# Moving the small tiles: weights at multiples of 512 bytes of a partition, turned activations 128 bytes beyond one

## Chip, cores and metric

The kernel runs on one core of one Trainium2 chip. The metric is the device time of one execution, in microseconds (us). All times of the kernel before come from three runs and from one profiled execution.

## What is computed

Two blocks of a network, each two layers deep, on 256 tokens of width 1024, in float32. The first block is an attention layer and a state-space (SSM) layer, each followed by a squared-ReLU MLP of width 4096. The second block has two layers, each a three-branch mixer followed by a mixture of 32 experts (MoE). Nearly all of the work is dense products of activations with weights that are read once from HBM:

```python
def first_block(x, ...):
    for i in range(DEPTH):
        mix = attention_mixer(...) if i % 2 == 0 else mamba2_bidir_mixer(...)
        x = layer_norm(DN_ALPHA * x + mix, ...)
        x = layer_norm(DN_ALPHA * x + jnp.square(jax.nn.relu(x @ w1)) @ w2, ...)

def second_block(x, c, positions, ...):
    for l in range(DEPTH):
        h = modulate(rms_norm(x, norm1_g[l]), sh1, sc1)
        x = x + gt1[:, None, :] * token_mixer(h, ...)
        h = modulate(rms_norm(x, norm2_g[l]), sh2, sc2)
        x = x + gt2[:, None, :] * hier_moe(h, ...)
    return rms_norm(x, final_g)
```

(The loops are written shorter here than in the reference.)

## The kernel before

**Stages.** The program runs attention, MLP 0, SSM, MLP 1, mixer 0, MoE 0, mixer 1, MoE 1 and the final norm, one after the other. `Stream` (`K.ws`) loads the weights of all stages in the order of use into a ring of five `raw` tiles of 1 MB. Outside the MoE each half of a `raw` tile is split into a high part `hi` (ScalarE, L160) and a rest `lo` (VectorE, L162), both of type float32r, in rings of seven tiles each. The activations are turned (transposed on TensorE, L368) and split in the same way by `tsplit` (L371, L372), into pairs that end in `h` and `l`.

**The two kinds of matmul.** A float32 product is made of three float32r matmuls: high by high, high by rest, rest by high.

- *Wide* ones (`mm3`, L266 to L268): 128 turned activations are loaded into the array (LDWEIGHTS) and up to 512 columns of a weight tile stream past them.
- *Narrow* ones (`b_half`, L339 to L341): 128 columns of a weight tile are loaded and 256 turned activations stream past.

Each matmul has a LDWEIGHTS of its own, and the one for the next matmul runs while the present matmul streams. So TensorE reads two places of SBUF at once: the one that streams and the one that is loaded. In the following, the *start* of a tile is its byte address in a partition modulo 512. All slices that these matmuls take of a tile begin at multiples of 512 bytes from the tile's own start (a few in the mixer at 256), so the start of the tile tells that of the slice. The *distance* is the difference of the two starts.

**Where the tiles lie.** Pools are laid out one after another in each partition, and every tile begins at a multiple of 32 bytes. Below the first pool lie 16384 bytes that the runtime keeps and four constants of 32 bytes each, so the first pool, the ring (L211 of the kernel before), begins 128 beyond a multiple of 512. `raw`, `hi` and `lo` have sizes that are multiples of 512 and keep that start. The pool `tail` (`self.tp`, L215) holds the tiles `th` and `tl` and behind them small tiles of the norms: `lnst` and `lnag` (L429, L430), `rstd` (L420) and `rss` (L1110, L1964). Behind it each stage opens a pool of its own, which begins 128 beyond a multiple of 512. In attention the row `sinkr` of 32 bytes lies ahead of the pair `xT` (L602, L606), in the mixer the row `fb` of 32 bytes (16 used; L1261, L1264), and so both pairs start at 160.

**Order of the work.** The program is written in the order of dependence, and a scheduler sets the order on each engine. The two loads `sinkr` and `fb` are DMAs that SyncE (SP) issues.

Of the kernel before, what the change touches and what calls it, by code (L numbers as in the profile page):

```python
# [10 lines left out]
F32 = mybir.dt.float32  # L11
# [19 lines left out]
class Job:  # L31
# [4 lines left out]
    def __init__(self, src, nk, ncol, nsplit, whole=False):  # L36
        self.src, self.nk, self.ncol, self.nsplit, self.whole = src, nk, ncol, nsplit, whole
        self.raw = None
        self.spare = self.pair = False
# [168 lines left out]
class Kern:  # L208
    def __init__(self, ctx, tc, ins, raw_bufs=5, split_bufs=7):
        self.ctx, self.tc, self.nc, self.I = ctx, tc, tc.nc, ins  # L210
        self.ring = ctx.enter_context(tc.tile_pool(name="ring", bufs=1, reuse_waits="tile"))  # L211
        self.cst = ctx.enter_context(tc.tile_pool(name="cst", bufs=1, reuse_waits="tile"))
        self.xp = ctx.enter_context(tc.tile_pool(name="xp", bufs=1, reuse_waits="tile"))
        self.rp = ctx.enter_context(tc.tile_pool(name="rows", bufs=1, reuse_waits="tile"))
        self.tp = ctx.enter_context(tc.tile_pool(name="tail", bufs=1, reuse_waits="tile"))  # L215
        self.ps = ctx.enter_context(tc.tile_pool(name="ps", bufs=1, space=PSUM))
        self.ready = {}
        self.finish = self.last = None
        self.held = 0
        self.actx = ExitStack()  # L220
        self.ws = Stream(self, raw_bufs, split_bufs)
        self.sides = []
# [193 lines left out]
    def rstd(self, var, eps, name="rstd"):  # L416

        nc = self.nc
        n = var.shape[1]
        r = self.tp.tile([128, 16], F32, name=name, tag=name, bufs=2)  # L420
        nc.vector.tensor_scalar(r[:, :n], var, eps, None, op0=OP.add)  # L421
        self.pow = nc.gpsimd.tensor_tensor(r[:, :n], r[:, :n], self.mhalf[:, :n], OP.pow).ins  # L422
        return r

    def layer_norm_tok(self, tok, P, g, b):

        nc = self.nc
        y = self.x[:, tok]
        st = self.tp.tile([128, 2, 6], F32, name="lnst", tag="lnst", bufs=2)  # L429
        ag = self.tp.tile([128, 2], F32, name="lnag", tag="lnag", bufs=2)  # L430
        for c in range(2):
            s = slice(c * 512, c * 512 + 512)
            nc.vector.scalar_tensor_tensor(y[:, s], y[:, s], ALPHA, P[c], op0=OP.mult, op1=OP.add)
            nc.vector.bn_stats(st[:, c], y[:, s])
        nc.vector.bn_aggr(ag, st)
        r = self.rstd(ag[:, 1:2], 1e-5)
        for c in range(2):
            s = slice(c * 512, c * 512 + 512)
            nc.vector.scalar_tensor_tensor(y[:, s], y[:, s], ag[:, 0:1], g[:, s], op0=OP.subtract, op1=OP.mult)
            i = nc.vector.scalar_tensor_tensor(y[:, s], y[:, s], r[:, 0:1], b[:, s], op0=OP.mult, op1=OP.add)  # L440
        self.last = i.ins
        return i.ins
# [151 lines left out]
def attn_layer(K):  # L594
    nc, tc, I, ws = K.nc, K.tc, K.I, K.ws
    with ExitStack() as ctx:
        p = ctx.enter_context(tc.tile_pool(name="att", bufs=1, reuse_waits="tile"))
# [1 line left out]
        c1 = p.tile([128, _C.shape[1] - nc1], F32, name="c1")  # L599
        nc.scalar.dma_start(c1, I["consts"][:, nc1:])  # L600
        win, rcos, rsin = (c1[:, _OFF[k][0] - nc1:_OFF[k][0] - nc1 + _OFF[k][1]] for k in ("win", "rcos", "rsin"))
        sinkr = K.load_row(p, I["attn_sink"][0], 8, "sinkr")  # L602
        K.place(p, ("sm", 2, 3, F32), ("smT", 2, 2, F32), ("nab", 4, 3, F32), ("ao", 8, 1, F32), ("qa", 4, 1, F32),
                ("qaT", 4, 1, F32), ("qbT", 4, 1, F32), ("kbT", 4, 1, F32), ("vb", 4, 1, F32))
        g, b = K.row(I["ln1_g"][0]), K.row(I["ln1_b"][0])
        xT = K.pair(p, 8, "xT")  # L606
        qa = p.tile([128, 2, 4, 2, 64], F32, name="qa")
        ka = p.tile([128, 2, 2, 64], F32, name="ka")
        va = p.tile([128, 2, 128], F32, name="va")
# [12 lines left out]
        for t in range(2):  # L622
            ct, st = rcos[:, t * 64:t * 64 + 64], rsin[:, t * 64:t * 64 + 64]
# [483 lines left out]
def rms_gain(K, tok, dst, sq, g, eps=1e-6):  # L1107

    nc = K.nc
    ss = K.tp.tile([128, 2], F32, name="rss", tag="rss", bufs=2)  # L1110
    K.squared = nc.scalar.activation(sq, K.x[:, tok], AF.Square, scale=D ** -0.5, accum_out=ss[:, 0:1]).ins
    for c in range(2):
        s = slice(c * 512, c * 512 + 512)
        K.gained = nc.vector.tensor_tensor(dst[:, s], K.x[:, tok, s], g[:, s], OP.mult).ins
    return K.rstd(ss[:, 0:1], eps)
# [132 lines left out]
def mixer_layer(K, l):  # L1248
    nc, tc, I, ws = K.nc, K.tc, K.I, K.ws
    with ExitStack() as ctx:  # L1250
        p = ctx.enter_context(tc.tile_pool(name="mix", bufs=1, reuse_waits="tile"))
# [6 lines left out]
                nc.sync.dma_start(shift, bass.AP(tensor=K.mod[l].tensor, offset=K.mod[l].offset, ap=[[0, 128], [1, D]]))  # L1258
        hn = p.tile([128, 2, D], F32, name="hn", tag="mg")
        K.place(p, ("gt", 4, 1, F32), ("rv", 4, 1, F32))  # L1260
        fb = K.load_row(p, I["fox_fb_2"][l], 4, "fb")  # L1261
        gq = K.load_row(p, I["mla_q_norm_g_2"][l], 256, "gq", tag="qpeT")
        gkv = K.load_row(p, I["mla_kv_norm_g_2"][l], 128, "gkv")
        hT = K.pair(p, 8, "xT")  # L1264

        def norm(t):
            tail = K.finish
            with ExitStack() as order:
                if t == 0:
                    order.enter_context(K.early(t, AHEAD))  # L1270
                elif tail:
                    order.enter_context(tc.issue_after(K.diag))
                    order.enter_context(tc.issue_after(K.turned))
                    tail(t)
                    K.finish = None
                r = rms_gain(K, t, hn[:, t], p.tile([128, D], F32, name="rsq", tag="yb"), gain)
                if t:
                    rms_scale(K, hn[:, t], r, shift)
                    K.tsplit(hn[:, t], hT, t, 0, 8)
                    end, turned = K.split  # L1280
                else:
                    with tc.issue_after(K.scattered) if l else nullcontext():
                        Ps = shift_pair(K, shift)
                    end = rms_pair(K, t, hn[:, t], r, shift, hT, p.tile([128, 8, 64], F32, name="dg", tag="rq", bufs=1)[:, 0:2].rearrange("p a b -> p (a b)"), Ps)
            if l == 0:
                K.release(t, end, turned if t else K.turned)
            elif tail:
                ws.limit = 1 << 30 if t else ws.limit + NEXT // 2
                with tc.issue_after(end), tc.issue_after(turned if t else K.squared):
                    ws.pump()  # L1290
# [19 lines left out]
        ss = p.tile([128, 4], F32, name="mss")  # L1310
# [4 lines left out]
        r = K.rstd(ss, 1e-6)  # L1315
# [636 lines left out]
def final_norm(K, dst):  # L1952
    nc = K.nc
    with ExitStack() as ctx:
        p = ctx.enter_context(K.tc.tile_pool(name="fin", bufs=1, reuse_waits="tile"))
        g = K.row(K.I["final_g_2"])
        o = p.tile([128, 2, D], F32, name="fo")
        c0, c1 = slice(0, 512), slice(512, 1024)
        for t in range(2):
            with K.tc.issue_after(i) if t else nullcontext():  # L1960
                if t and K.finish:
                    K.finish(t)
                    K.finish = None
                ss = K.tp.tile([128, 2], F32, name="rss", tag="rss", bufs=2)  # L1964
                nc.scalar.activation(p.tile([128, D], F32, name="rsq", tag="rsq", bufs=2), K.x[:, t], AF.Square, scale=D ** -0.5,  # L1965
                                     accum_out=ss[:, 0:1])
                i = nc.vector.tensor_tensor(o[:, t, c0], K.x[:, t, c0], g[:, c0], OP.mult).ins  # L1967
                r = K.rstd(ss[:, 0:1], 1e-6)
            nc.scalar.activation(o[:, t, c0], o[:, t, c0], AF.Identity, scale=r[:, 0:1])
            nc.vector.scalar_tensor_tensor(o[:, t, c1], K.x[:, t, c1], r[:, 0:1], g[:, c1], op0=OP.mult, op1=OP.mult)  # L1970
            for c in (c0, c1):
                nc.sync.dma_start(dst[0, t * 128:t * 128 + 128, c], o[:, t, c])
# [9 lines left out]
def program(ctx, tc, ins, out, phases=ALL, opts=None):  # L1982
# [24 lines left out]
    if "attn" not in phases:  # L2007
        with tc.tile_pool(name="set2", bufs=1) as p:
            setup2(K, p)
    run = {"attn": lambda: attn_layer(K), "mlp0": lambda: mlp_layer(K, 0), "mlp1": lambda: mlp_layer(K, 1), "ssm": lambda: ssm_layer(K),  # L2010
           "mix0": lambda: mixer_layer(K, 0), "mix1": lambda: mixer_layer(K, 1), "ada": lambda: ada_alone(K),
           "moe0": lambda: moe_layer(K, 0), "moe1": lambda: moe_layer(K, 1), "fin": lambda: final_norm(K, out)}
    for ph in phases:
        run[ph]()
# [32 lines left out]
```

## Time and profile before

| what | us |
|---|---|
| median of 3 runs | 2350.51 |
| lowest and highest | 2349.61, 2353.59 |
| the profiled execution, its own time | 2345.05 |
| its span, first to last instruction | 2343.3 |

| engine | busy us | share of the span |
|---|---|---|
| PE (matmul) | 2198.4 | 94% |
| PEld (weight load) | 1510.0 | 64% |
| DVE | 1180.4 | 50% |
| ACT | 811.4 | 35% |
| POOL | 118.7 | 5% |

The shares are averages over stages of different kinds; a matmul's recorded duration reaches into the next one, since matmuls are pipelined. How often matmuls start is read from the start times of the timeline, and not from a mean duration. The mean granted clock of TensorE was 0.987 of full speed.

### The profile page before, as it was taken

To read this page: it belongs to the slowest core of one execution; us is meant where nothing else is said; L and a number is where in the kernel's file an instruction comes from. 1 tells how busy PE (TensorE), PEld (TensorE's weight loads), DVE (VectorE), ACT (ScalarE), POOL (GpSimd) and SP (SyncE) were. 2 spreads that over 40 slices of the span, in tenths; PEclk is the share of its full clock that TensorE was granted. 3 is DMA by queue.
4 is the path that set the end of the run, shared out by engine and by line. 5 is a ranking of instruction groups with operands and counts; after the bars stand their busy time and mean duration, and the time that the engine had idled before them with its cause. 6 is when DMAs were issued, how large, how long until landed. Compare 5 with 4: busy or idle time off the path is not lost. (4 is left out here: it accounts for less than half of the span.)

```text
span 2343.3 us, 30480 instructions
## 1 busy us (share of the span) xinstructions
PE 2198.4 (94%) x11877; PEld 1510.0 (64%) x11877; DVE 1180.4 (50%) x2024; ACT 811.4 (35%) x1404; POOL 118.7 (5%) x98
## 2 busy tenths in 40 slices
PE   8999999998999999999999988889999899888887
PEld 7878889997888888874444443348877544443333
DVE  6589978997998756652111111036665411111113
ACT  5544446775444444431111111115443211111111
POOL 0000002222000000110000000000001000000000
PEclk9999999999999999998999999989999999999999
DMA  9379855434898554677999999985566899999997
GB/s 332 110 252 359 305 158 153 130 132 141 305 347 299 179 162 161 226 240 290 375 393 395 394 394 394 393 314 193 170 207 208 316 362 395 395 395 393 393 394 268
DMA packets 307105, 669.11 MB, mean 286 GB/s; under 512 B 20996, under 2 KB 60780, under 8 KB 306952
## 3 DMA queue, kind: packets, MB, share of 16 engines
q1 hardware_dynamic: 299496, 663.56, 78.2%
q10 hardware_dynamic: 7456, 3.49, 0.6%
q8 instruction: 97, 1.59, 0.3%
q14 instruction: 56, 0.46, 0.1%
HBM read 665.90 MB, written 1.10 MB: 285 GB/s over the span
## 5 line engine op out<-in xcount | busy, mean ns | idle before, releaser
L162 DVE TENSOR_TENSOR lo<-raw,hi 128x1024 fp32r<-128x1024 f32 (+2 forms) x353 | 433.5, 1236 | 184.5 <-ACT hi L160 183.1
L160 ACT ACTIVATE hi<-raw 128x1024 fp32r<-128x1024 f32 (+2 forms) x353 | 369.6, 1056 | 340.9 <-PE acc L268 224.9
L1712 PE MATMUL acc<-raw,XT 128*64 128x512 f32 x1248 | 366.5, 603 | 76.0 <-DMA raw<-in_exp_w 75.9
L1712 PEld LDWEIGHTS acc<-raw,XT 128*64 128x64 f32 x1248 | 109.8, 138 | 311.4 <-issue 179.3
L266 PE MATMUL acc<-hi,xTh 128*128 128x512 f32 (+2 forms) x608 | 229.5, 379 | 4.9 <-ACT xTh L371 2.4
L1712 PE MATMUL acc<-pre,XT 128*64 128x512 f32 x784 | 231.8, 597 | 0.0
L1727 DVE TENSOR_TENSOR aT<-s,acc 128x256 f32<-128x256 f32 x60 | 25.1, 422 | 410.3 <-ACT s L1725 409.8
L267 PE MATMUL acc<-lo,xTh 128*128 128x512 f32 (+2 forms) x608 | 226.6, 373 | 0.0
L268 PE MATMUL acc<-hi,xTl 128*128 128x512 f32 (+2 forms) x608 | 225.1, 374 | 0.4 <-DVE xTl L1150 0.3
L1740 PE MATMUL pb<-pre,aT 128*64 128x512 f32 x928 | 208.7, 594 | 0.0
L1764 DVE SCALAR_TENSOR_TENSOR Yl<-pb,wcol,Yh 128x512 fp32r<-128x512 f32 x56 | 40.2, 748 | 296.9 <-ACT Yh L1763 296.0
L1717 ACT ACTIVATE H<-acc 128x512 f32<-128x512 f32 x64 | 38.2, 597 | 382.4 <-PE acc L1712 382.4
L1740 PEld LDWEIGHTS pb<-pre,aT 128*64 128x64 f32 x928 | 80.3, 137 | 123.3 <-issue 115.3
L339 PE MATMUL acc<-xTh,hi 128*128 128x256 f32 x456 | 130.6, 287 | 2.9 <-DVE ca L895 2.9
L266 PEld LDWEIGHTS acc<-hi,xTh 128*128 128x128 f32 x608 | 115.5, 190 | 26.7 <-ACT xTh L371 4.1
L340 PE MATMUL acc<-xTl,hi 128*128 128x256 f32 x456 | 129.9, 285 | 0.0
L341 PE MATMUL acc<-xTh,lo 128*128 128x256 f32 x456 | 129.5, 285 | 0.0
L339 PE MATMUL pb<-xTh,hi 128*128 128x256 f32 x448 | 126.8, 285 | 1.4 <-ACT hi L160 1.4
L267 PEld LDWEIGHTS acc<-lo,xTh 128*128 128x128 f32 x608 | 115.5, 190 | 19.4 <-DVE lo L162 0.8
L268 PEld LDWEIGHTS acc<-hi,xTl 128*128 128x128 f32 x608 | 114.6, 190 | 20.6 <-DVE xTl L372 1.1
L340 PE MATMUL pb<-xTl,hi 128*128 128x256 f32 x448 | 126.7, 283 | 0.0
L422 POOL TENSOR_TENSOR rstd<-rstd,mhalf 128x1 f32<-128x1 f32 (+2 forms) x36 | 30.4, 845 | 1901.5 <-DVE rstd L421 1858.1
(493 smaller groups left out, 3920.0 us busy)
## 6 DMA issues: line engine op xcount, KB each, us to landing
pre<-in_exp_w SPq DMA_DIRECT2D x428, 512.0 KB
raw<-in_exp_w SPq DMA_DIRECT2D x160, 1024.0 KB
raw<-in_mlp_w SPq DMA_DIRECT2D x64, 1024.0 KB
adaw<-in_ada_w SPq DMA_DIRECT2D x96, 512.0 KB
raw<-in_w_in SPq DMA_DIRECT2D x24, 1024.0 KB
raw<-in_gate_w SPq DMA_DIRECT2D x24, 1024.0 KB
raw<-in_ssm_w_in SPq DMA_DIRECT2D x16, 1024.0 KB
raw<-in_branch_w SPq DMA_DIRECT2D x12, 1024.0 KB
```

The lines of the kernel that those rows point to most:

```text
L160: nc.scalar.activation(hi[:, :size], flat, AF.Copy)
L162: eng.tensor_tensor(lo[:, :size], flat, f32(hi[:, :size]), OP.subtract)
L266: nc.tensor.matmul(P, ah, bh, start=start, stop=False)
L267: nc.tensor.matmul(P, ah, bl, start=False, stop=False)
L268: nc.tensor.matmul(P, al, bh, start=False, stop=stop)
L339: nc.tensor.matmul(P, wh, xh[:, k + kk], start=first and start and kk == 0, stop=False, skip_group_check=True)
L340: nc.tensor.matmul(P, wh, xl[:, k + kk], start=False, stop=False, skip_group_check=True)
L341: nc.tensor.matmul(P, wl, xh[:, k + kk], start=False, stop=stop and kk == n - 1, skip_group_check=True)
L1712: K.pe = nc.tensor.matmul(P[64 * o:64 * o + 64], XT[G][1][k][:, i], hs[2 * o + u].raw[:, kk], start=(k == 0), stop=(k == 7)).ins
L1717: nc.scalar.activation(H[e], P, AF.Copy)
L1740: K.pe = nc.tensor.matmul(PY[c][64 * o:64 * o + 64], aT[2 * n + o][:, f], hs[2 * o + u].raw[:, 0, cs], start=(f == 0), stop=(f == 3)).ins
L1764: nc.vector.scalar_tensor_tensor(Y[j][1][:, cs], PY[c], wcol[:, j:j + 1], f32(Y[j][0])[:, cs], op0=OP.mult, op1=OP.subtract)
```

## The change

A pool `small` is opened ahead of the ring and takes the small tiles of the norms out of `tail`. It is 384 bytes long, so the ring begins at a multiple of 512, and the pools of the stages stay where they were, since `tail` is shorter by the same 384 bytes. In attention and in the mixer the pair `xT` is allocated ahead of the 32-byte row. No computation is added or taken away.

```diff
 class Kern:
+        self.sp = ctx.enter_context(tc.tile_pool(name="small", bufs=1, reuse_waits="tile"))
+        self.place(self.sp, ("lnst", 12 / 256, 2, F32), ("lnag", 2 / 256, 2, F32), ("rstd", 16 / 256, 2, F32), ("rss", 2 / 256, 2, F32))
         self.ring = ctx.enter_context(tc.tile_pool(name="ring", bufs=1, reuse_waits="tile"))
...
     def rstd(self, var, eps, name="rstd"):
-        r = self.tp.tile([128, 16], F32, name=name, tag=name, bufs=2)
+        r = self.sp.tile([128, 16], F32, name=name, tag=name, bufs=2)
...
     def layer_norm_tok(self, tok, P, g, b):
-        st = self.tp.tile([128, 2, 6], F32, name="lnst", tag="lnst", bufs=2)
-        ag = self.tp.tile([128, 2], F32, name="lnag", tag="lnag", bufs=2)
+        st = self.sp.tile([128, 2, 6], F32, name="lnst", tag="lnst", bufs=2)
+        ag = self.sp.tile([128, 2], F32, name="lnag", tag="lnag", bufs=2)
...
 def attn_layer(K):
-        sinkr = K.load_row(p, I["attn_sink"][0], 8, "sinkr")
         K.place(p, ("sm", 2, 3, F32), ("smT", 2, 2, F32), ("nab", 4, 3, F32), ("ao", 8, 1, F32), ("qa", 4, 1, F32),
                 ("qaT", 4, 1, F32), ("qbT", 4, 1, F32), ("kbT", 4, 1, F32), ("vb", 4, 1, F32))
+        xT = K.pair(p, 8, "xT")
+        sinkr = K.load_row(p, I["attn_sink"][0], 8, "sinkr")
         g, b = K.row(I["ln1_g"][0]), K.row(I["ln1_b"][0])
-        xT = K.pair(p, 8, "xT")
...
 def mixer_layer(K, l):
-        fb = K.load_row(p, I["fox_fb_2"][l], 4, "fb")
         gq = K.load_row(p, I["mla_q_norm_g_2"][l], 256, "gq", tag="qpeT")
         gkv = K.load_row(p, I["mla_kv_norm_g_2"][l], 128, "gkv")
         hT = K.pair(p, 8, "xT")
+        fb = K.load_row(p, I["fox_fb_2"][l], 4, "fb")
```

`rss` moves to the new pool in `rms_gain` and in `final_norm` in the same way. The starts of the tiles in the two built programs:

| tile | before | changed |
|---|---|---|
| weights `raw`, `hi`, `lo` | 128 | 0 |
| `xT` of attention and of both mixers | 160 | 128 |
| `th`, `tl` (odd MLP slices, attention out, mixer branches and out) | 256 | 128 |
| `hT` and `xT` of the MLPs | 128 | 128 |
| `xT` of the SSM layer | 256 | 256 |
| `x`, `row` | 256 | 128 |
| activations of the experts (`XT`, `aT`, `OHT`) | 224, 480 | 224, 480 |

And the float32r matmuls by the starts of what streams and what is loaded, counted in the built programs:

| matmuls | activations | weights | distance before | distance after |
|---|---|---|---|---|
| 1200 wide (attention, mixers) | 160 to 128 | 128 to 0 | 32 | 128 |
| 924 wide (`th`, `tl`, and 48 with `row`) | 256 to 128 | 128 to 0 | 128 | 128 |
| 480 wide (MLPs) | 128 | 128 to 0 | 0 | 128 |
| 96 wide of 452 columns (mixers) | 160 to 128 | 128 to 0 | 32 | 128 |
| 96 wide (SSM out) | 256 | 128 to 0 | 128 | 256 |
| 1344 narrow (MLPs) | 128 | 128 to 0 | 0 | 128 |
| 576 narrow (attention, mixers) | 160 to 128 | 128 to 0 | 32 | 128 |
| 792 narrow and 384 wide of 256 columns (SSM) | 256 | 128 to 0 | 128 | 256 |

(Some 150 others of smaller shapes are left out; most of them keep the distance 128.)

On PE, DVE, ACT and POOL the instructions of the two programs stand in the same order, row for row. Only SP's queue differs, at the head of each mixer; here at mixer 0, where `sh` is a row of the modulation, and `gq`, `gkv` and `fb` are rows that VectorE multiplies with or adds. Before:

```order
L91 DMA raw<-in_w_in 128x4x512 x4
L1258 DMA sh<-mod_80 128x1024
L393 DMA fb<-in_fox_fb 128x4
L393 DMA gq<-in_mla_q_norm_g 128x256
L393 DMA gkv<-in_mla_kv_norm_g 128x128
L399 DMA row<-in_gate_b 128x1024
```

And in the changed program:

```order
L91 DMA raw<-in_w_in 128x4x512 x4
L1260 DMA sh<-mod_87 128x1024
L395 DMA gq<-in_mla_q_norm_g 128x256
L395 DMA gkv<-in_mla_kv_norm_g 128x128
L395 DMA fb<-in_fox_fb 128x4
L401 DMA row<-in_gate_b 128x1024
```

`fb` now stands behind `gq` and `gkv`; the load of `sinkr` keeps its place.

## Rows read from the trace of the kernel before

**Rows 1.** The page: busy us of TensorE, share of the span, instructions.

```profile
PE 2198.4 (94%) x11877; PEld 1510.0 (64%) x11877; DVE 1180.4 (50%) x2024; ACT 811.4 (35%) x1404; POOL 118.7 (5%) x98
```

**Rows 2.** Busy us by stretch (instructions), then granted clock, DMA share, GB/s.

```profile
60.00:1020.00 960.00, 940.73 (x5755) 813.97 (x5754) 770.75 (x1199) 490.82 (x821) 86.61 (x69) 0.99 0.62 213
1080.00:1540.00 460.00, 421.86 (x2000) 186.19 (x1996) 75.36 (x138) 68.15 (x143) 0.00 (x0) 1.00 1.04 390
1560.00:1800.00 240.00, 237.31 (x1235) 194.17 (x1232) 155.31 (x298) 115.86 (x176) 19.28 (x15) 0.99 0.58 196
1860.00:2330.00 470.00, 427.77 (x2030) 188.69 (x2026) 76.20 (x140) 68.93 (x145) 0.00 (x0) 1.00 1.02 383
```

**Rows 3.** Groups by line and shape: count, busy us, mean ns, idle before.

```profile
L266 PE MATMUL acc<-hi,xTh 128*128 128x512 f32 x432 | 174.8, 406 | 4.2 <-ACT xTh L371 1.6 <-ACT xTh L374 1.6 <-ACT hi L160 0.9
L266 PE MATMUL acc<-hi,th 128*128 128x512 f32 x292 | 115.9, 398 | 1.4 <-ACT th L371 1.4
L266 PE MATMUL acc<-hi,hTh 128*128 128x512 f32 x128 | 49.4, 391 | 0.0
L339 PE MATMUL acc<-xTh,hi 128*128 128x256 f32 x456 | 130.6, 287 | 2.9 <-DVE ca L895 2.9
L339 PE MATMUL pb<-xTh,hi 128*128 128x256 f32 x448 | 126.8, 285 | 1.4 <-ACT hi L160 1.4
```

**Rows 4.** Timeline, MLP 1, wide, distance 0: start us, us, instruction.

```profile
722.00 0.40 PE L266 MATMUL acc<-hi,hTh 128*128 128x512 f32 x1
...
732.91 0.28 PE L339 MATMUL pb<-xTh,hi 128*128 128x256 f32 x1
```

**Rows 5.** Timeline, MLP 1, wide, distance 128.

```profile
746.41 0.39 PE L266 MATMUL acc<-hi,th 128*128 128x512 f32 x1
...
757.56 0.28 PE L339 MATMUL pb<-xTh,hi 128*128 128x256 f32 x1
```

**Rows 6.** Timeline, mixer 0, wide, distance 32.

```profile
1004.14 0.39 PE L266 MATMUL acc<-hi,xTh 128*128 128x512 f32 x1
...
1015.34 0.39 PE L266 MATMUL acc<-hi,th 128*128 128x512 f32 x1
```

**Rows 7.** Timeline, MLP 1, narrow, distance 0.

```profile
685.79 0.28 PE L339 MATMUL pb<-xTh,hi 128*128 128x256 f32 x1
...
697.31 0.39 PE L266 MATMUL acc<-hi,th 128*128 128x512 f32 x1
```

**Rows 8.** Timeline, mixer 0, narrow, distance 32.

```profile
813.21 0.28 PE L339 MATMUL acc<-xTh,hi 128*128 128x256 f32 x1
...
835.62 0.38 PE L1333 MATMUL pb<-call,kpe 128*128 128x128 f32 x2
```

**Rows 9.** Timeline, SSM, narrow, distance 128: weights loaded, activations stream.

```profile
506.65 0.28 PE L339 MATMUL acc<-xTh,hi 128*128 128x256 f32 x1
...
510.68 0.59 PE L945 MATMUL pb<-xo,cbo 128*128 128x256 f32 x2
```

**Rows 10.** Timeline, SSM, wide of 256 columns, distance 128: activations loaded, weights stream.

```profile
360.09 0.28 PE L266 MATMUL acc<-hi,xTh 128*128 128x256 f32 x1
...
365.66 0.28 PE L268 MATMUL acc<-hi,xTl 128*128 128x256 f32 x1
```

**Rows 11.** Tile `fb`: its DMA and its reader, durations ns, first and last start us.

```profile
L393 SPq DMA_DIRECT2D fb<-in_fox_fb x2: 347/394/442, 782.8 to 1564.0; - x2
L1301 DVE TENSOR_TENSOR fvv<-ms,fb x2: 159/160/160, 815.5 to 1591.9; 128x8 f32<-128x8 f32 x2
```

**Rows 12.** Timeline, MLP 0, wide, distance 128: one long step.

```profile
180.99 0.40 PE L268 MATMUL acc<-hi,tl 128*128 128x512 f32 x1
181.23 0.40 PE L266 MATMUL acc<-hi,th 128*128 128x512 f32 x1
```

**Rows 13.** DMA queues at 6.4 to 7.4 us, then 43 to 47: packets, MB, share.

```profile
q1 hardware_dynamic: 104, 0.36, 96.8%
...
q1 hardware_dynamic: 431, 1.64, 102.8%
```

More of the change, by code (lines that the diff above doesn't have):

```diff
@@ L1109, in rms_gain @@
     nc = K.nc
-    ss = K.tp.tile([128, 2], F32, name="rss", tag="rss", bufs=2)
+    ss = K.sp.tile([128, 2], F32, name="rss", tag="rss", bufs=2)
     K.squared = nc.scalar.activation(sq, K.x[:, tok], AF.Square, scale=D ** -0.5, accum_out=ss[:, 0:1]).ins
@@ L1963, in final_norm @@
                     K.finish = None
-                ss = K.tp.tile([128, 2], F32, name="rss", tag="rss", bufs=2)
+                ss = K.sp.tile([128, 2], F32, name="rss", tag="rss", bufs=2)
                 nc.scalar.activation(p.tile([128, D], F32, name="rsq", tag="rsq", bufs=2), K.x[:, t], AF.Square, scale=D ** -0.5,
```

## The prediction

> **What bounds the kernel now.** First the page: TensorE is busy for 94% of the span, nearly twice as long as VectorE [rows 1]. Then busy time by stretch, since the stages have different limits [rows 2]. Two kinds of stage show. From 60 to 1020 us (attention, the MLPs, the SSM, mixer 0) and from 1560 to 1800 (mixer 1) TensorE is busy for 98 to 99% of the time at a granted clock of 0.99, while the DMA engines have a share of 0.62 and 0.58. There a matmul that starts later moves the end. From 1080 to 1540 and from 1860 to 2330 (the two MoE stages) the DMA share is 1.04 and 1.02, and TensorE is busy for 91 to 92%: the weights' transfer sets the pace there, and what TensorE gains in these 930 us is lost in waiting for weights.
>
> Then the groups by line and shape give the counts [rows 3]. Their mean durations are no help here: a wide matmul is recorded with 391 to 406 ns though the next one starts after some 230. So the price of a matmul is taken from the timeline, from the start of a block to the start of what follows it, over blocks in which TensorE never stopped. I chose one block for each distance of the two starts:
>
> - Wide, 512 columns. Distance 0, `hTh` and `hTl` of MLP 1: 48 matmuls in 732.91 - 722.00 = 10.91 us, 227.3 ns each [rows 4]. Distance 128, `th` and `tl` in the same stage: 48 in 757.56 - 746.41 = 11.15 us, 232.3 ns [rows 5]. Distance 32, `xT` of mixer 0: 48 in 11.20 us, 233.3 ns [rows 6].
> - Narrow, 256 columns. Distance 0, MLP 1: 96 in 11.52 us, 120.0 ns [rows 7]. Distance 32, mixer 0: 192 in 22.41 us, 116.7 ns [rows 8]. Distance 128, SSM: 34 in 4.03 us, 118.5 ns [rows 9].
> - The SSM also has wide matmuls of 256 columns, where the roles are swapped: the weights, at 128, stream and the activations, at 256, are loaded. From the first start to the 48th it is 5.57 us for 47 steps, 118.5 ns [rows 10].
>
> At the granted clock of 0.99 to 1.00 [rows 2], which is the level of 2.4 GHz, 512 columns take 213.3 ns and 256 take 106.7, so 10 to 20 ns of each step are lost, and how many depends on where the two operands lie. That is the whole of what this change can touch. Two readings of these blocks matter for it. First, rows 4 and 5 come from one stage with the same weights in the same tiles, and differ by 5.0 ns, so the places do count. Second, rows 9 and 10 have the same distance with the roles exchanged, once the weights and once the activations at the multiple of 256, and give the same 118.5 ns. I take from this that the distance counts, and not which operand is at the rounder address.
>
> **The change part by part.** No instruction is added or taken away, and the order on PE, DVE, ACT and POOL is the same. What moves is addresses and one small DMA per mixer.
>
> *Wide matmuls.* With the distance as the cause, all that come to a distance of 128 cost 232.3 ns [rows 5]. 1200 leave 32: 1200 x (232.3 - 233.3) = -1.2 us. 480 leave 0: 480 x (232.3 - 227.3) = +2.4 us. 924 stay at 128: 0. The 96 of 452 columns go from 32 to 128, for which I take the same -1.0 ns: -0.1 us.
>
> *Narrow matmuls.* 1344 leave 0: 1344 x (118.5 - 120.0) = -2.0 us. 576 leave 32: 576 x (118.5 - 116.7) = +1.0 us.
>
> *The SSM.* Its `xT` keeps 256 while the weights move to 0, so 1176 matmuls of 256 columns and 96 of 512 go to a distance of 256, which the trace does not show. The nearest rows are those of the other three distances: 116.7 to 120.0 ns [rows 7, 8], so from 1176 x -1.8 = -2.1 us to 1176 x 1.5 = +1.8 us, and 96 x 5 = 0.5 us either way. I take 0, the middle.
>
> *The moved DMA.* `fb` goes behind `gq` and `gkv` on SP's queue. It is issued at 782.8 us and read first at 815.5 [rows 11]. The rows ahead of it take about 1 us of issue, so it has some 31 us to spare, and costs 0; with this cover gone it would be 1 us per mixer.
>
> *The other engines and the transfers.* `raw`, `hi` and `lo` move together, as do `x` and `row`, so ScalarE and VectorE see the same distances as before. They are busy for 51 and 80% of the first stretch [rows 2] and run under TensorE. The transfers of weights now land at multiples of 512. For this the trace has a pair: the rows of `x` land at a multiple of 256 and need 0.968 x 16 us / 0.36 MB = 43 us of engine time per MB, the rows of `raw` at 128 need 1.028 x 64 / 1.64 = 40 us [rows 13]. Landing at the rounder address is not cheaper, so I take 0.
>
> Sum: -1.2 + 2.4 - 0.1 - 2.0 + 1.0 + 0 = +0.1 us, all of it in stages that TensorE bounds. The profiled execution took 2345.05 us and would take 2345.2. The median of the runs is 2350.51, 5.5 us above the profiled one, so the forecast is 2350.6 us. About 0.2% (4.7 us) is what a measurement of this kernel can tell from no change.
>
> **A rule against the trace.** Two blocks that differ in nothing but the place of the loaded operand start their matmuls every 227.3 and every 232.3 ns [rows 4, 5]. The Trainium skill, "TensorE: Matmul & The Clock Gate", section "Part 2: What happens when you issue a matmul", says that TensorE has two independent read ports, so that loading the next weights takes no read bandwidth from the running matmul. By that rule each term above would be 0 and the sum 0.0 instead of +0.1 us; the trace disagrees with it by the 5.0 ns.
>
> **The rivals.**
>
> *The multiple of 512 counts by itself.* No block of the trace has an operand that begins at a multiple of 512. If it is this that spares TensorE its losses (an operand that begins there crosses one boundary fewer), then wide matmuls fall to the best level seen, 227.3 ns, and narrow ones to 116.7. Wide: 1200 x 6.0 + (924 + 96) x 5.0 = 12.3 us. Narrow size: 1344 x 3.3 + 1176 x 1.8 = 6.5 us. That gives 2350.5 - 18.8 = 2331.7 us; with the wide ones alone 2338.2. For it: that the levels differ at all by a few ns shows that places cost something, and only this one was never tried. Against it: the equal 118.5 ns in rows 9 and 10, where a multiple of 256 gave nothing to either operand. Chance 0.25.
>
> *The long step becomes the rule (slower).* In blocks at distance 128 single steps are long: 181.23 - 180.99 = 240 ns [rows 12] against the mean of 232.3. If weights that stream from a multiple of 512 fall into the long step each time, the wide matmuls cost 1200 x 6.7 + (924 + 96) x 7.7 + 480 x 12.7 = 22.0 us, which gives 2372.5 us. It decides from a mean wide step of 234.0 ns on (4.7 us over 2700 matmuls is 1.7 ns). For it: at distance 128 and 32 the steps vary, and the MLPs, now the most even, lose their distance of 0. Against it: 924 matmuls have had the distance 128 all along, at 232.3 ns. Chance 0.14.
>
> *The transfers get shorter.* If each packet of weights cost an additional piece for beginning 128 bytes beyond a multiple of 256, the MoE stages would gain. A packet of 2048 bytes with 128 more would be 5.9% longer, and 5.9% of 930 us is 55 us, for 2295.8 us. The Trainium skill says so of descriptors, that their pieces must start at multiples of 256 bytes and that what is fetched ahead of the start costs time ("DMA: Bandwidth & Descriptors", section "How a descriptor splits into AXI transactions"); it gives the reading side, and the trace does not bear it out for where data lands, with 43 us per MB against 40 [rows 13]. Chance 0.03.
>
> *The change does not do what it says everywhere.* In the SSM the turned activations stay 256 beyond. This is in the forecast, with its bounds of -2.6 to +2.3 us.
>
> **How the numbers follow.** Forecast (distance alone) 0.56, the multiple of 512 0.25, the long step 0.14, transfers 0.03, and 0.02 for a loss I have not thought of. Of the forecast's 0.56 some 0.05 lie over 4.7 us away (0.03 faster, 0.02 slower). Faster: 0.25 + 0.03 + 0.03 = 0.31. Slower: 0.14 + 0.02 + 0.02 = 0.18. Same: 0.51. The likeliest case alone, with the SSM's bounds and the 3 us between runs, lies in 2346 to 2355. The range reaches down to the first rival, 2331.7, a little beyond it to 2330, and up to 2358, where a third of the long steps would be. That leaves out most of the slower rival, the transfers and the deepest part of the first rival, about 0.2.
>
> **What the profile after would show.** Right: in MLP 1 the `hTh` blocks at 232 ns a step and the narrow ones at 118 to 119, both mixers' wide blocks at 232 to 233, the SSM's at 117 to 120, the MoE stages as long as before at a DMA share over 1.0. The first rival shows as wide blocks of 227 or less everywhere, `th` included. The second shows as wide steps of 235 to 240. The third shows as MoE stages that move clearly more than the 390 GB/s of rows 2. The forecast is wrong if `th` blocks, whose distance does not change, change their step: then the distance is not the cause.

## The result and the profile after

| kernel | median us | runs | lowest, highest |
|---|---|---|---|
| before | 2352.05 | 4 | 2349.61, 2354.75 |
| changed | 2320.72 | 4 | 2312.87, 2324.26 |

The ratio is 0.9868, with a 95% interval of 0.9851 to 0.9885: 31 us faster. The forecast was 2350.6 us with a range down to 2330, so the result lies below the range. The profiled execution of the changed kernel took 2312.87 us, its span is 2311.0, and its mean granted clock is 0.988 against 0.987 before.

TensorE is not where the time went. Its line of the page, which answers to [rows 1], has 6.9 us less of busy time:

```profile
PE 2191.5 (95%) x11877; PEld 1514.7 (66%) x11877; DVE 1180.6 (51%) x2024; ACT 811.3 (35%) x1404; POOL 118.7 (5%) x98
```

Where it went is read from instructions that stand once or a few times in the program: the product with `kpe` in the two mixers (first and last start), and the first and last up product of the MoE stages. Before (duration ns, then first and last start in us):

```profile
L1333 PE MATMUL pb<-call,kpe x4: 270/271/272, 835.6 to 1611.3; 128*128 128x128 f32 x4
L1712 PE MATMUL acc<-raw,XT x1248: 592/592/1114, 1071.1 to 2316.7; 128*64 128x512 f32 x179
```

And in the changed kernel, where every line number is higher by 2:

```profile
L1335 PE MATMUL pb<-call,kpe x4: 270/271/275, 839.0 to 1591.7; 128*128 128x128 f32 x4
L1714 PE MATMUL acc<-raw,XT x1248: 592/592/1057, 1071.2 to 2283.3; 128*64 128x512 f32 x179
```

At mixer 0 the changed kernel is 3.4 us *behind* (839.0 against 835.6). At the first up product of MoE 0 the two are level (1071.2 and 1071.1). At mixer 1, so after MoE 0, it is 19.6 us ahead, and at the last up product of MoE 1 33.4. The whole gain comes from the stretches with the MoE stages in them. Both traces have the same 11877 matmuls in the same order, so they can be set side by side one by one: from 1038 to 1575 us and from 1814 us to the end (times of the kernel before) the changed kernel is 22.7 and 12.5 us shorter, and the rest of the program is 3.0 us longer. Some 3 of the 22.7 us belong to these two executions and not to the change: at the head of MoE 0, from 1038 to 1075 us, the granted clock was 0.72 before and 0.91 in the changed kernel. In the repetition of the change (experiment 6) it was 0.72 there too, and the two stretches are 19.1 and 12.7 us shorter.

Those are bound by the transfers [rows 2]. Busy time by stretch, from the middle of each MoE stage; the columns are the stretch, its length, busy us of PE, PEld, DVE, ACT and POOL (with the number of instructions), and last the granted clock, the DMA share and GB/s. Before:

```profile
1150.00:1480.00 330.00, 300.64 (x1416) 132.99 (x1416) 50.47 (x94) 47.34 (x99) 0.00 (x0) 0.99 1.04 394
1950.00:2250.00 300.00, 271.79 (x1268) 119.15 (x1270) 45.46 (x83) 41.88 (x87) 0.00 (x0) 0.99 1.04 394
```

Changed:

```profile
1150.00:1480.00 330.00, 310.29 (x1490) 139.47 (x1489) 51.32 (x96) 49.61 (x105) 0.00 (x0) 1.00 1.04 411
1950.00:2250.00 300.00, 276.49 (x1304) 124.16 (x1302) 45.86 (x84) 43.21 (x91) 0.00 (x0) 1.00 1.04 411
```

The DMA engines are as full as before, 1.04, and move 411 GB/s in place of 394. The queues of the same 330 us say the same per packet (packets, MB, share of 16 engines). Before, then changed:

```profile
q1 hardware_dynamic: 56176, 129.68, 104.2%
```

```profile
q1 hardware_dynamic: 58294, 135.53, 104.1%
```

A MB needed 1.042 x 16 x 330 us / 129.68 = 42.4 us of engine time and now needs 40.6, 4.4% less. In the records of single packets (which the trace keeps beside the views shown here), those of 2048 bytes took 88.6 ns on average and now 84.1, those of 4096 took 163.5 and now 159.4: 4 to 4.5 ns less for a packet of either size. It is not the same amount for each packet: before, nearly all of 2048 bytes took between 84 and 95 ns, and now 43835 of 43871 take exactly 84. What TensorE gains from it is the wait for `raw` in the MoE (page, costliest groups: busy us, mean ns, idle time before and what ended it). Before, then changed:

```profile
L1712 PE MATMUL acc<-raw,XT 128*64 128x512 f32 x1248 | 366.5, 603 | 76.0 <-DMA raw<-in_exp_w 75.9
```

```profile
L1714 PE MATMUL acc<-raw,XT 128*64 128x512 f32 x1248 | 359.4, 598 | 50.5 <-DMA raw<-in_exp_w 49.9
```

In the stages that TensorE bounds, the steps can be set beside rows 4 to 9. Timeline of the changed kernel, first instruction of a block and first one behind it (start us, us, instruction):

```profile
298.84 0.28 PE L341 MATMUL pb<-xTh,hi 128*128 128x256 f32 x1
...
310.36 0.40 PE L268 MATMUL acc<-hi,hTh 128*128 128x512 f32 x1
...
509.34 0.28 PE L341 MATMUL acc<-xTh,hi 128*128 128x256 f32 x1
...
513.41 0.38 PE L947 MATMUL pb<-xo,cbo 128*128 128x256 f32 x1
...
556.49 0.62 PE L270 MATMUL acc<-hi,xTl 128*128 128x512 f32 x2
...
564.44 0.60 PE L947 MATMUL pb<-xo,cbo 128*128 128x256 f32 x2
...
688.60 0.28 PE L341 MATMUL pb<-xTh,hi 128*128 128x256 f32 x1
...
700.00 0.39 PE L268 MATMUL acc<-hi,th 128*128 128x512 f32 x1
...
724.66 0.40 PE L268 MATMUL acc<-hi,hTh 128*128 128x512 f32 x1
...
735.86 0.28 PE L341 MATMUL pb<-xTh,hi 128*128 128x256 f32 x1
...
749.27 0.39 PE L268 MATMUL acc<-hi,th 128*128 128x512 f32 x1
...
760.41 0.28 PE L341 MATMUL pb<-xTh,hi 128*128 128x256 f32 x1
...
815.99 0.28 PE L341 MATMUL acc<-xTh,hi 128*128 128x256 f32 x1
...
839.03 0.38 PE L1335 MATMUL pb<-call,kpe 128*128 128x128 f32 x2
...
1007.39 0.40 PE L268 MATMUL acc<-hi,xTh 128*128 128x512 f32 x1
...
1018.59 0.40 PE L268 MATMUL acc<-hi,th 128*128 128x512 f32 x1
...
1024.20 0.38 PE L370 MATMUL pb<-call,mg 128*128 128x128 f32 x2
```

The last product of the SSM stage (SSM out, wide) before:

```profile
553.89 0.39 PE L268 MATMUL acc<-hi,xTl 128*128 128x512 f32 x1
...
562.01 0.38 PE L945 MATMUL pb<-xo,cbo 128*128 128x256 f32 x1
```

| block | matmuls | distance before, after | ns a step before | after |
|---|---|---|---|---|
| wide, `hTh` of MLP 1 [rows 4] | 48 | 0, 128 | 227.3 | 11.20 us / 48 = 233.3 |
| wide, `th` of MLP 1 [rows 5] | 48 | 128, 128 | 232.3 | 11.14 / 48 = 232.1 |
| wide, `xT` of mixer 0 [rows 6] | 48 | 32, 128 | 233.3 | 11.20 / 48 = 233.3 |
| wide, SSM out | 35 | 128, 256 | 232.0 | 7.95 / 35 = 227.1 |
| narrow, MLP 1 [rows 7] | 96 | 0, 128 | 120.0 | 11.40 / 96 = 118.8 |
| narrow, MLPs [rows 7; after: MLP 0] | 96 | 0, 128 | 120.0 | 11.52 / 96 = 120.0 |
| narrow, mixer 0 [rows 8] | 192 | 32, 128 | 116.7 | 23.04 / 192 = 120.0 |
| narrow, SSM [rows 9] | 34 | 128, 256 | 118.5 | 4.07 / 34 = 119.7 |

One block is not all blocks of its kind. In the kernel before, the MLPs' blocks at distance 0 agree within half a ns (wide `hTh` 227.2 to 227.6, narrow 119.6 to 120.0). At 128 they do not: in the changed kernel the narrow blocks of the MLPs take some 118.7 ns in places and 120.0 in others, the `hTh` blocks 232.1 to 233.3 (the one in the table is among the slowest), and `th` in mixer 0, which had 232.1 ns at the same distance before, takes (1024.20 - 1018.59) / 24 = 233.8.

So TensorE lost a little and the transfers gave 4.4%. Two things had to be told apart: which of the moved tiles shortens the packets, and by what (the place where they land, or TensorE's reads of that place).

### The profile page after: what moved, and what is told of

The parts are those of the page before. It is cut to its first block, busy times and chain, and to the rows that moved or that the text cites. A ratio compares the mean times of both kernels' runs of the same rounds, so it can differ in the third digit from the quotient of the medians.

```text
span 2311.0 us, 30480 instructions
## 1 busy us (share of the span) xinstructions
PE 2191.5 (95%) x11877; PEld 1514.7 (66%) x11877; DVE 1180.6 (51%) x2024; ACT 811.3 (35%) x1404; POOL 118.7 (5%) x98
## 5 line engine op out<-in xcount | busy, mean ns | idle before, releaser
L1714 PE MATMUL acc<-raw,XT 128*64 128x512 f32 x1248 | 359.4, 598 | 50.5 <-DMA raw<-in_exp_w 49.9
```

What stands on the lines that cost most here:

```text
L1714: K.pe = nc.tensor.matmul(P[64 * o:64 * o + 64], XT[G][1][k][:, i], hs[2 * o + u].raw[:, kk], start=(k == 0), stop=(k == 7)).ins
```

## The experiments

**1. The small pool behind the ring.** The weights keep their start of 128, all else is as in the change.

```diff
-        self.sp = ... "small" ...; self.place(self.sp, ...)
         self.ring = ctx.enter_context(tc.tile_pool(name="ring", ...))
         self.cst = ctx.enter_context(tc.tile_pool(name="cst", ...))
+        self.sp = ... "small" ...; self.place(self.sp, ...)
```

> Edit: the changed kernel, but with the small pool opened behind the ring and the constants instead of ahead of the ring. The weights then keep their old start of 128, while all the rest is as in the change (xT, th, tl, x, row at 128). Theory A (the start at which the weights land makes their packets short when the DMA engines are saturated): the MoE stages stay at 394 GB/s as before the change, and none of the 30 us is there. Theory B (moving the small tiles, x, row, th, tl or the reorder of xT did it): the MoE stages move 411 GB/s. For TensorE, by the distance of the two operands: weights and turned activations all lie at 128, so every wide matmul comes to distance 0 and 227.3 ns; 1200 x 6.0 + 924 x 5.0 + 96 x 6.0 = 12.4 us less, narrow ones 576 x (120.0 - 116.7) = 1.9 us more, together 10.5 us faster than before (about 2341.5 us beside 2352). If only a start at a multiple of 512 helped TensorE, its steps stay at 232 to 233 ns and the time is that of before within 0.2%.

Measured: 2343.82 us (12 runs) beside 2351.69, ratio 0.9969 (0.9954 to 0.9983). The MoE stays at 394 GB/s, and the mixer's wide block takes 10.88 us / 48 = 226.7 ns a step:

```profile
1150.00:1480.00 330.00, 301.34 (x1414) 132.64 (x1412) 49.01 (x90) 46.87 (x99) 0.00 (x0) 0.99 1.04 394
```

```profile
1000.13 0.39 PE L268 MATMUL acc<-hi,xTh 128*128 128x512 f32 x1
...
1011.01 0.39 PE L268 MATMUL acc<-hi,th 128*128 128x512 f32 x1
```

Theory A holds, and B falls: neither the small tiles nor `x`, `row`, `th`, `tl` nor `xT` shorten the packets. The gain of 7.3 us (4.0 to 10.8) comes with no operand at a multiple of 512. The wide steps at the distance of 0 give it, 10.5 us by the expected sum; 4.0 us of it stand already at the wide block of mixer 0 (1000.13 against 1004.14 [rows 6]).

**2. The small pool without the reorder.** The rows `sinkr` and `fb` stand ahead of `xT` again.

```diff
-        xT = K.pair(p, 8, "xT")
         sinkr = K.load_row(p, I["attn_sink"][0], 8, "sinkr")
+        xT = K.pair(p, 8, "xT")
```

> Edit: the changed kernel without its reorder, so sinkr and fb stand ahead of xT again (xT at 160) and the weights begin at 0. Theory A (landing start of the weights): MoE at 411 GB/s, and the whole gain is there, 2320 us within some 5 us; wide matmuls of attention and mixers at the distance of 160 (not seen so far), at 227 to 234 ns: within -7 and +2 us of the changed kernel. Theory B (the reorder of xT did it): MoE at 394 GB/s and about 2350 us.

Measured: 2320.14 us (4 runs), ratio 0.9866 (0.9842 to 0.9889), and in the queue's row of 1150 to 1480 us as much as in the change:

```profile
q1 hardware_dynamic: 58833, 135.45, 104.1%
```

The reorder has no part in the gain. Experiments 1 and 2 together leave the start of the weights. (`raw`, `hi` and `lo` moved together in every run, and the MoE loads into all three, so they were not told apart. The pool of the constants, which lies behind the ring and moved with it, is at its old start of 128 in experiment 7, where the rate is 411 GB/s all the same.)

**3. Half of the up product left out, in the kernel before.**

```diff
-                    for kk in range(2):
+                    for kk in range(1):
...
-                                                    start=(k == 0), stop=(k == 7)).ins
+                                                    start=(k == 0), stop=(k == 6)).ins
```

> Edit to the kernel before: in the MoE stages every second matmul of the up product is left out (half of the rows of the two up matrices are loaded but not multiplied), so that TensorE reads half as much of the up weights while as much lands. Theory A1 (the landing start by itself lengthens the packets): MoE stages stay at 394 GB/s with the weights at 128, and the time is that of before within 10 us, since the transfers set the pace. Theory A2 (TensorE's reads of the weights at 128 get in the way of the transfers' writes): with two thirds of the reads left, the rate rises by about a third of the 17 GB/s, to 400 or more, some 10 us or more off the two MoE stages.

Measured: one run, 2337.51 us. TensorE's busy time in the stretch falls from 300.64 to 268.38 us, and the rate does not move:

```profile
1150.00:1480.00 330.00, 268.38 (x1036) 112.48 (x1034) 47.82 (x88) 45.67 (x96) 0.00 (x0) 0.89 1.04 394
```

So A1: with 27% fewer matmuls in the stretch the packets are as long as before, and TensorE's reads do not lengthen them by anything that shows. That the time fell by 14 us, more than A1's 10, comes from outside this stretch. The two profiled executions differ by 7.6 us of span (2335.7 against 2343.3; the one of before was itself 7 us below its median), and from 1030 to 1150 us, at the edge of MoE 0 where the DMA share is 0.92 and 0.89, the kernel with half of the product moves 338 GB/s in place of 319.

**4. Weights at 256, and 5. at 192.** Only `lnst` (128 bytes), or only `lnag` (64 bytes), goes ahead of the ring; the other small tiles stay in `tail`.

```diff
-        self.place(self.sp, ("lnst", ...), ("lnag", ...), ("rstd", ...), ("rss", ...))
+        self.place(self.sp, ("lnst", 12 / 256, 2, F32))
```

> Edit: only lnst goes to the pool ahead of the ring, so that the weights begin at 256 instead of 0 (xT stays at 128, so the distance is 128 as in the change; th and tl at 384, distance 128 too). If a multiple of 256 is enough for the short packets: MoE at 411 GB/s and 2320 us. If it has to be a multiple of 512: MoE at 394 GB/s and about 2352 us. If the packet pays by how far it begins behind the multiple of 512: something else, such as 400 GB/s.

Measured: 2316.37 us (4 runs), ratio 0.9854 (0.9831 to 0.9877). The queue's row:

```profile
q1 hardware_dynamic: 58347, 135.53, 104.1%
```

A multiple of 256 is enough; the multiple of 512 that the change aims at is not needed for this.

> Edit: only lnag goes ahead of the ring, so that the weights begin at 192 (xT at 128, distance 64; th and tl at 320, distance 128). If the packets pay once for any start that is no multiple of 256: MoE at 394 GB/s as with 128. If they pay by how far the start is from the next multiple of 256: some 400 GB/s or more. If a multiple of 64 that is none of 128 costs more: under 394. A distance of 64 was not seen so far; between those of 32 and 128 it would be 232 to 233 ns wide and 117 to 118 narrow.

Measured: one run, 2338.64 us, and the queue's row is that of before:

```profile
q1 hardware_dynamic: 56085, 129.69, 104.1%
```

At 64 bytes short of a multiple of 256 the packets pay as much as at 128 (42.4 us for a MB both times, 88.6 and 163.5 ns a packet). So of the four starts that ran, 0 and 256 are free, and 128 and 192 cost the same. The Trainium skill, "DMA: Bandwidth & Descriptors", section "How a descriptor splits into AXI transactions", states this boundary of 256 for reading, and experiments 4 and 5 agree with it for landing. By an estimate in that section's beats of 32 bytes, a packet of 2048 would take 68 in place of 64 from a start of 128 and 70 from 192; the runs show no difference between these two.

The 12 us that this one run is nevertheless below the 2350.73 of before are not from the MoE's rate. By the profiles it is 7.9 us ahead at the first up product of MoE 0 already (1063.2 against 1071.1), so most of them are TensorE's. Its wide steps at the distance of 64, expected at 232 to 233 ns, are 229 in the mixers' `xT` blocks. Its narrow steps were a surprise. Two blocks of MLP 0:

```profile
270.11 0.28 PE L341 MATMUL pb<-xTh,hi 128*128 128x256 f32 x1
...
281.41 0.39 PE L268 MATMUL acc<-hi,th 128*128 128x512 f32 x1
...
294.57 0.28 PE L341 MATMUL pb<-xTh,hi 128*128 128x256 f32 x1
...
305.46 0.39 PE L268 MATMUL acc<-hi,hTh 128*128 128x512 f32 x1
```

96 in 11.30 us are 117.7 ns, and 96 in 10.89 us 113.4, at the same distance of 64. So the distance is not all of it; what sets the second block apart from the first stays open.

**6. The change again, and 7. all at 0.** The comparison first:

> The changed kernel as it is, as the comparison for the other kernels on the same chip: 2320 us, MoE stages at 411 GB/s.

Measured: 2321.08 us (5 runs), ratio 0.9866 (0.9845 to 0.9887). Then the kernel with the distance of 0 and the start of 0:

```diff
+        self.cst = ctx.enter_context(tc.tile_pool(name="cst", ...))
         self.sp = ctx.enter_context(tc.tile_pool(name="small", ...))
-        self.place(self.sp, ("lnst", ...), ("lnag", ...), ("rstd", ...), ("rss", ...))
+        self.place(self.sp, ("sml", 16 / 256, 2, F32), ("rstd", 16 / 256, 2, F32))
         self.ring = ctx.enter_context(tc.tile_pool(name="ring", ...))
-        self.cst = ctx.enter_context(tc.tile_pool(name="cst", ...))
```

> Edit: the constants and a small pool of 256 bytes (lnst, lnag and rss share one tile) are opened ahead of the ring, so that the weights and also x, row, th, tl, xT of attention and mixers, hT and xT of the MLPs begin at 0; xT of the SSM at 128. Theory D (landing at a multiple of 256 sets the transfers, the distance of the operands sets TensorE, and the two are independent): MoE at 411 GB/s as in the change, and in the other stages 2700 wide matmuls x (227.3 - 232.3) = -13.5 us, 1920 narrow ones x (120.0 - 118.5) = +2.9 us, SSM 1176 x (118.5 - 119.7) + 96 x (232.3 - 227.5) = -0.9 us: 11.5 us less than the change, about 2309 us. Rival (TensorE's step depends on the weights' start and not on the distance): as the change, 2320 us.

Measured: 2307.67 us (5 runs), ratio 0.9826 (0.9805 to 0.9847), 13.4 us below the change where 11.5 were expected. The MoE moves 411 GB/s, and the mixer's wide block takes 10.88 us / 48 = 226.7 ns:

```profile
1150.00:1480.00 330.00, 310.33 (x1482) 139.47 (x1478) 49.90 (x92) 49.13 (x105) 0.00 (x0) 1.00 1.04 411
```

```profile
683.12 0.28 PE L341 MATMUL pb<-xTh,hi 128*128 128x256 f32 x1
...
694.63 0.40 PE L268 MATMUL acc<-hi,th 128*128 128x512 f32 x1
...
999.34 0.39 PE L268 MATMUL acc<-hi,xTh 128*128 128x512 f32 x1
...
1010.22 0.39 PE L268 MATMUL acc<-hi,th 128*128 128x512 f32 x1
```

The two effects add, as Theory D has it: the steps went to those of the distance of 0 while the rate stayed. The start of 0 gives TensorE nothing that the start of 128 in experiment 1 did not: 226.7 ns both times.

**8. `xT` of the MLPs at 32, and 9. at 64 (with that of the SSM).** The narrow block above, at distance 0, takes 11.51 us / 96 = 119.9 ns; rows 8 have 116.7 at distance 32.

```diff
+        K.place(p, ("pad0", 8 / 256, 1, F32))
         xT = K.pair(p, 8, "xT")
+        K.place(p, ("pad1", 120 / 256, 1, F32))
```

> Edit: as the kernel with all at 0, but xT of the MLPs begins at 32, with 480 bytes behind it so that hT stays at 0. By the distance: 1344 narrow matmuls x (116.7 - 120.0) = -4.4 us, and 96 wide ones that also load xT x (233.3 - 227.3) = +0.6 us: 3.8 us less than with all at 0, about 2305 us. If the 120.0 and 116.7 ns of the two stages had another cause: the same as all at 0.

Measured: 2304.63 us (5 runs), ratio 0.9808 (0.9791 to 0.9826): 3.0 us below all at 0, about the 3.8 expected, but within both intervals. The step is as expected, 11.20 us / 96 = 116.7 ns:

```profile
684.58 0.28 PE L341 MATMUL pb<-xTh,hi 128*128 128x256 f32 x1
...
695.78 0.40 PE L268 MATMUL acc<-hi,th 128*128 128x512 f32 x1
```

For the next two, all at 0 ran again on the same chip:

> The kernel with all at 0 as it is, as the comparison for the next two on the same chip: 2308 us.

Measured: 2309.89 us (5 runs), ratio 0.983 (0.9814 to 0.9846). With a `pad0` of 64 bytes, and one of 448 ahead of `xT` in the SSM:

> Edit: as the kernel with all at 0, but xT of the MLPs and of the SSM begin at 64 (hT stays at 0), so that nearly all narrow matmuls come to the distance of 64, which took 116.7 ns a step in the run with the weights at 192 (MLPs; 119.6 in the SSM), against 120.5 and 120.9 with all at 0. If the distance of 64 is what counts: 1344 x (116.7 - 120.5) + 792 x (119.6 - 120.9) + 384 x (118.9 - 121.7) = -7.2 us, about 2301 us. If it was the start of 192 itself: within 2 us of all at 0.

Measured: 2305.64 us (5 runs), ratio 0.9814 (0.9801 to 0.9827), 4.3 us below all at 0 in place of 7.2, and again within both intervals. The same block takes 11.31 us / 96 = 117.8 ns:

```profile
687.76 0.28 PE L341 MATMUL pb<-xTh,hi 128*128 128x256 f32 x1
...
699.07 0.39 PE L268 MATMUL acc<-hi,th 128*128 128x512 f32 x1
```

That is the slower of the two levels in experiment 5. The expected 116.7 was a mean over both.

**10. Longer packets.** If packets set the pace of the MoE, fewer and longer ones must help.

```diff
-    up = lambda e: [rows(w[e], k, 4, 0, 512, whole=True) for k in (0, 4) for w in (w1, w3)]
+    up = lambda e: [Job([w[e][k * 128:(k + 4) * 128].rearrange("(u p k) n -> p u (k n)", p=128, k=2)], 2, 1024, 2, True)
+                    for k in (0, 4) for w in (w1, w3)]
...
-                    ds = slice(d * 128, d * 128 + 128)
+                    ds = slice(d // 2 * 256 + d % 2, d // 2 * 256 + 256, 2)
```

> Edit: as the kernel with the distance of 64, and the up weights of the MoE are loaded with two neighbouring rows per partition, 4096 contiguous bytes in place of two times 2048, with the gathered activations in the matching order. If the MoE stages are bound by packets (84.1 ns for 2048 bytes, 159.4 for 4096): the packets of two thirds of the bytes take 5.2% less, the rate goes from 411 to about 426 GB/s, and the two stages of some 440 us each lose 3.5%, 31 us: about 2270 us. If TensorE, which is busy for 94% there, becomes the bound first: a part of it, between 2271 and 2300 us. Rival: nothing, if the rate of 411 GB/s is a limit of its own and not the packets' time.

Measured: 2291.38 us (5 runs), ratio 0.9755 (0.9738 to 0.9772), 14.3 us below the kernel with the distance of 64 and the fastest of all. Stretch and queue:

```profile
1150.00:1480.00 330.00, 312.51 (x1504) 143.00 (x1500) 51.39 (x94) 50.33 (x106) 0.00 (x0) 1.00 1.03 420
```

```profile
q1 hardware_dynamic: 37091, 138.23, 102.3%
```

A MB takes 1.023 x 5280 / 138.23 = 39.1 us of engine time, 3.7% less than 40.6 and what was expected. But the share fell from 104.1 to 102.3%, so the rate rose only to 420 GB/s, 2.2%, and the time by half of the 31 us. The rival (411 as a limit of its own) falls. The other case of the expectation, that TensorE becomes the bound, would also have given a time between 2271 and 2300 us, but the DMA engines are full all through this stretch, so the transfers still set the pace. Why the share fell was not tested. An estimate from the two queues' rows: the share above 100% is 0.041 x 5280 us / 58294 = 3.7 ns a packet in the changed kernel and 0.023 x 5280 / 37091 = 3.3 ns here. If an engine's packets overlap by that much each, fewer packets have less overlap, and some 40% of what the longer ones save is lost by it.

## Why the prediction was wrong

- **The transfers: the step that failed.** It is "Landing at the rounder address is not cheaper, so I take 0", with the 0.03 for the rival "The transfers get shorter". Landing at a multiple of 256 made a MB 4.4% cheaper in the MoE stages (42.4 to 40.6 us of engine time), and that is the whole gain: experiments 1, 2, 4 and 5 show that the start of the weights does it. The rival named this condition and its place. Its size was too large: 5.9% is right as the share of 128 bytes in 2176 (of 2048 they are 6.25%), but the measured 4.5 ns are 5.1% of a packet of 2048 bytes and 2.5% of one of 4096. In place of 55 us on all of the 930 us it gave 32 to 35 us over the two stretches, also because they are not full of transfers from end to end: the share is 1.04 in the middle and 0.89 from 1030 to 1150 us.
- **The rival's mechanism: not borne out.** One additional piece in each packet would cost each packet the same, wherever it lands off a multiple of 256. From 840 to 940 us of the kernel before, at a DMA share of 0.45, all packets of 2048 bytes are weights that land at 128, and 5600 of 6144 take the 84 ns of the start of 0. In the full stretch they spread from 84 to 95. So the price shows only where the engines are full, and varies from packet to packet. What lengthens them there stays open.
- **Why rows 13 misled.** Their pair, `x` against `raw`, stands on 1 and 4 us of the trace. Nearly all bytes of both are in packets of 4096 bytes, 89 and 397 of them. The median of `x` is 159 ns and a few long packets raise its mean to 172; `raw` has a median and a mean of 164. So `x` looked dearer by an average that its typical packet does not have. Nor could this pair have told the price: in the changed kernel `x` lands at 128, and the same window has a median of 159 and a mean of 172 again, while `raw`, now at 0, has fallen from a median of 164 to 159. Where the engines have gaps, the start does not show. Queues from 560 to 640 us, before and changed:

```profile
q1 hardware_dynamic: 7401, 21.12, 73.2%
```

```profile
q1 hardware_dynamic: 7519, 20.76, 71.5%
```

  That is 44.4 and 44.1 us for a MB, 0.6% apart, where it is 4.4% in the MoE. So I took the price from a stretch that this price does not rule. The same rows 2 that name the transfers as the bound of 930 us show where a change of the landing place had to be judged.
- **The distance: right for most of it, not for all.** Wide steps went where it says: 227.3 to between 232.1 and 233.3 for `hTh`, no change for `th` in MLP 1, and back to 226.7 when experiments 1 and 7 set it to 0. The first rival ("The multiple of 512 counts by itself") falls, since experiment 1 has the fast steps with no operand at such a multiple. But the prediction's own sign against the distance was a `th` block that changes its step, and those of the mixers did, from 232.1 to 233.8 ns in the block shown. With the two levels of narrow blocks at 64 and at 128, it says that at these distances something else counts for 1 to 4 ns. What it is was not found. The wide product at 256 (SSM out), which no row showed before, takes 227.1 ns, as at 0.
- **Its sizes: off by a few us.** Summed over matched steps without a wait in either trace, the MLPs' narrow ones went by -0.6 us in place of -2.0, those of attention and mixers by +1.5 in place of +1.0, the wide ones that left 0 by +2.1 in place of +2.4, those that left 32 by -0.4 in place of -1.2. The SSM, taken as 0, lost 1.0 us in its matmuls of 256 columns and gained 0.3 in its wide ones. In place of +0.1 us, the program was 3.3 us behind at the end of mixer 0 (1007.39 against 1004.14 [rows 6]); some 1.1 us of that stand at 28 us already, after attention's first wide block, in which TensorE waits.
- **The long step: no.** It was to decide from a mean wide step of 234.0 ns on. The slowest blocks, `th` of the mixers, came to 233.8, the others to 233.4 or less.
- **The range.** It was built on TensorE's terms alone. With the transfers at 0.03, 2330 looked wide; the bound that rules 40% of the span had a range of zero.

## What to carry over

Judge a change of addresses for each engine in the stretch that this engine bounds: a row from a stretch with gaps says nothing of a full one. Let weights land at multiples of 256 bytes of a partition where transfers bound the time, and keep what streams and what is loaded at the same start modulo 512 for wide matmuls (226.7 to 227.3 ns a step against 232 to 234), some 32 bytes apart for narrow ones (116.7 against 119.9 at the same start). When packets set the pace, doubling the length of the short ones gives more on top of the right start.

## What was not expected of the hardware

- In the full stretch a packet costs 4 to 4.5 ns more on average when its place begins at 128 or 192 modulo 512, whether it has 2048 or 4096 bytes; at 0 and at 256 it does not. Where the engines have gaps it costs nothing at 128 either: 84 ns for 5600 of 6144 packets at a share of 0.45.
- Two profiled executions of the same kernel (all at 0: experiment 7, then its repetition) differ by 6.3 us of span, 2301.8 and 2308.1, and it shows where the granted clock fell in one of them, with TensorE as busy as in the other:

```profile
540.00:650.00 110.00, 104.44 (x592) 87.76 (x591) 91.21 (x115) 54.65 (x84) 11.52 (x10) 1.00 0.70 250
```

```profile
540.00:650.00 110.00, 104.44 (x546) 87.22 (x545) 85.76 (x112) 49.49 (x80) 12.76 (x10) 0.94 0.64 226
```

  Terms of a few us are therefore compared block by block, and not by the spans of two profiles.
- With fewer matmuls in the MoE (experiment 3) the granted clock fell there from 0.99 to 0.89, a mixture of the two levels, and the transfers' rate did not notice.
